# Pair steps of a four-round MLP dealt out by a timetable, with transposes moved into the next product

## The chip, the cores and the metric

The kernel runs on one core of a Trainium2 chip. The metric is the time of one execution on the device in microseconds (us); a row of runs is given by its median. A core has five engines that run side by side and wait for each other through semaphores: TensorE (matmuls and weight loads; PE and PEld in the profile), VectorE (DVE), ScalarE (ACT), GpSimd (POOL) and SyncE (SP), whose queue issues nearly all loads here. Each engine takes its instructions strictly in the order that was fixed when the program was built.

## The reference

Two layers of a decoder trunk for 256 tokens of width 2048, in float32:

```python
D_MODEL = 2048; SEQ = 256; DEPTH = 2; D_FF = 4 * D_MODEL
# each layer
h = rms(x, norm1_g)
z = h @ w_in                      # u | retention q,k,v,g | NSA | differential attention
x = x + concat([s5(u), retention(...), nsa(...), diff_attn(...)]) @ w_out
h2 = rms(x, norm2_g)
x = x + relu(h2 @ mlp_w1) ** 2 @ mlp_w2      # 2048 -> 8192 -> 2048
```

The change lies in the last line, the MLP.

## The kernel before

**Products.** The precision of float32 is kept with the type fp32r: each operand is split into a high part (a copy rounded on ScalarE) and a low part (VectorE subtracts the high part), and three matmuls stand for one: low x high, high x high, high x low. Weights come in chunks of 128 x 1024 (two blocks of 128 rows by 512 columns, 512 KB). `split_chunk` loads a chunk into one of four buffers `raw` (SP), writes `wh` (three buffers, ScalarE) and `wl` (two buffers, VectorE). `product_steps` gives a chunk 12 matmuls of 512 columns: for each of the two row blocks and each half of the tokens (t = 0, 1) two with `wh` and one with `wl`. Eight chunks make a product of 2048 rows by 512 columns in two accumulators of PSUM, `mm` (pool `ps`, four banks; the pool `pm` has four more, tag `ms`).

**The MLP.** It goes in four rounds. A round makes four blocks of 512 hidden columns from `h2` and `w1` (`first` half), transposes them into the slots `Bh`, `Bl` (`to_slots`: TensorE transposes 128 x 128, ScalarE writes `Bh`, VectorE writes `Bl`), and multiplies these slots with its quarter of `w2` in four output products (`second`), whose sums `residual` adds to x.

**Pairs.** Two of the four blocks of a round are made together with seven products in place of eight (Strassen's scheme in a form with few additions): `first_steps` makes the two that need no sums (accumulators p1, p2; 6 matmuls for each of 8 chunks), `sums_steps` the other five (p3 to p7; 15 matmuls for each of 8 steps). A step of `sums_steps` loads a chunk of each of the two blocks, subtracts them four times (`t13`, `t24`), and splits three results into `bh`/`bl`, `t13h`/`t13l`, `t24h`/`t24l`: ten instructions of VectorE and ScalarE for 15 matmuls. The sums of `h2` that these multiply were made once (`sums_slot`). `pair_last` combines the seven accumulators into four tiles. The other two blocks of a round are plain products.

**The order before.** `mix` runs two generators side by side. In round 0 the pair's 8 steps go between the 16 chunks of the two plain blocks, one to two chunks. In rounds 1 to 3 they go between the 32 chunks of the preceding round's output products, one to four chunks; then the pair is combined and transposed, and the two plain blocks follow, each with its Relu, Square and transposes at its end. The last round's output products run alone. A pair of blocks is made in every round.

The framework places instructions by priority: what is written inside `self.hp()` counts as if written 350 instructions earlier, and each engine's order is fixed when the program is built. `lhs[k]`, `h2`, `kt2` and `kh` are the transposed left sides. Names in the profile leave out buffer numbers; `p` stands for all of p1 to p7, `t` for `t13` and `t24`, `mo`, `c`, `v` for tiles of the mixers and of `pair_last`.

Of the kernel before, what the change touches and what calls it, by code (L numbers as in the profile page):

```python
# [54 lines left out]
class Trunk:  # L55
# [107 lines left out]
    def product_steps(self, out, chunks, lhs, n=512, before=None):  # L163
# [5 lines left out]
        for c, src in enumerate(chunks):  # L169
            if before:  # L170
                before(c)
            wh, wl = self.split_chunk(src, 2 * n, not before)
            mov = lambda w, j: w[:, j * n:(j + 1) * n]
            rows = lambda x, t: x[:, t * P:(t + 1) * P]
            for j in range(2):
                k = 2 * c + j
                xh, xl = lhs[k]
                for t in range(NT):
                    nc.tensor.matmul(acc[t], rows(xl, t), mov(wh, j), start=k == 0, stop=False)  # L179
                    nc.tensor.matmul(acc[t], rows(xh, t), mov(wh, j), start=False, stop=False)  # L180
            for j in range(2):
                k = 2 * c + j
                for t in range(NT):
                    nc.tensor.matmul(acc[t], rows(lhs[k][0], t), mov(wl, j), start=False, stop=k == nk - 1)  # L184
            if c == len(chunks) - 1:
                out.extend(acc)
            yield
# [50 lines left out]
    def sums_steps(self, out, chunks1, chunks2, slots, sums):  # L238
# [3 lines left out]
        acc = {i: self.pm.tile([P, 512], F32, name=f"p{i}", tag="ms") for i in (6, 7, 5, 3)}  # L242
        acc[4] = self.ps.tile([P, 512], F32, name="p4", tag="mm")
        last = len(chunks1) - 1
        f2 = lambda x: x.rearrange("p a b -> p (a b)")
        for c in range(last + 1):
            with self.hp():
                b1 = self.raw(chunks1[c]).rearrange("p (k n) -> p k n", k=2)
                b2 = self.raw(chunks2[c]).rearrange("p (k n) -> p k n", k=2)
                ta, tb = (self.wk.tile([P, 2, 512], F32, name=nm, tag="aux", bufs=2) for nm in ("t13", "t24"))  # L250
                V.tensor_tensor(ta[:, 0, :], b2[:, 0, :], b1[:, 0, :], ALU.subtract)  # L251
                V.tensor_tensor(ta[:, 1, :], b2[:, 1, :], b2[:, 0, :], ALU.subtract)  # L252
                V.tensor_tensor(tb[:, 0, :], b2[:, 1, :], ta[:, 0, :], ALU.subtract)
                V.tensor_tensor(tb[:, 1, :], tb[:, 0, :], b1[:, 1, :], ALU.subtract)  # L254
                bh = self.wk.tile([P, 512], F32R, name="bh", tag="z")
                bl = self.wk.tile([P, 512], F32R, name="bl", tag="w")
                ah = self.wp.tile([P, 1024], F32R, name="t13h", tag="wh", bufs=3)
                al = self.wp.tile([P, 1024], F32R, name="t13l", tag="wl", bufs=2)
                dh = self.wk.tile([P, 1024], F32R, name="t24h", tag=("Tq", "Tk")[c % 2], bufs=1)
                dl = self.wk.tile([P, 1024], F32R, name="t24l", tag=("s5b", "vones")[c % 2], bufs=1)  # L260
                for h, l, x in ((bh, bl, b2[:, 1, :]), (ah, al, f2(ta)), (dh, dl, f2(tb))):
                    nc.scalar.activation(h, x, AF.Copy)  # L262
                    V.tensor_tensor(l, x, h.bitcast(F32), ALU.subtract)  # L263
            half = lambda y, i: [v[:, i * 512:(i + 1) * 512] for v in y]
            S = lambda i: [x[:, i, :] for x in sums[c]]
            f = (c == 0, c == last)
            self.three(acc[3], S(3), (bh, bl), *f)
            self.three(acc[5], S(0), half((ah, al), 0), *f)
            self.three(acc[7], S(2), half((ah, al), 1), *f)
            self.three(acc[6], S(1), half((dh, dl), 0), *f)  # L270
            self.three(acc[4], [x[:, 1, P:] for x in slots[c]], half((dh, dl), 1), *f)
            if c == last:
                out.update(acc)
            yield
# [16 lines left out]
    def to_slots(self, src, cols, slots, j0, gain=None, sums=None, bank=None):  # L291

        nc = self.nc
        for jj in range(cols // 256):
# [9 lines left out]
            else:  # L304
                self.split_slot(pt, slots[j0 + jj], gain, 2 * (j0 + jj))
# [735 lines left out]
    def mlp(self, layer, h2, sums, r, ss, last):  # L1041


        nc = self.nc
        V = nc.vector
        kt2 = self.ktiles(h2)
        w1 = lambda rd, n: [self.ins["w1"][layer, 4 * rd + n, c] for c in range(8)]
        bank = lambda name: self.ps.tile([P, 512], F32, name=name, tag="mm")
        tmp = lambda nm, tag, n: self.wk.tile([P, 512], F32, name=nm, tag=tag, bufs=n)
        nxt = [None]  # L1050

        def mix(xs, ys, every, off):
            for i, _ in enumerate(xs):
                if i % every == off:
                    next(ys, None)
            for _ in ys:
                pass

        def pair_first(rd):
            p = []  # L1060
            for _ in self.first_steps(p, w1(rd, 0), h2):
                pass
# [48 lines left out]
        def both(gens):  # L1111
            for g in gens:
                yield from g
# [153 lines left out]
```

## Time and profile before

| | |
|---|---|
| median of 3 runs | 2340.57 us (2339.39 to 2343.62) |
| profiled execution: time, span in the trace | 2340.26 us, 2338.5 us |
| mean granted clock of TensorE | 0.991 |
| TensorE, VectorE, ScalarE busy | 97%, 72%, 53% of the span |
| loads | 439 MB, 189 GB/s over the span |
| first MLP, second MLP | about 430 to 1176 us, 1589 to 2335 us |

The busy time of an engine is the union of its instructions' spans. Matmuls overlap in the array, so that one of 512 columns has a span of 0.39 us while the next starts earlier; a busy TensorE is not one at its peak. The granted clock is a mean over the two levels that TensorE can have, 1.2 and 2.4 GHz (0.5 and 1.0).

### The profile page before, as it was taken

What the parts mean: (1) busy time and instruction counts of PE and PEld (TensorE: products, weight loads), DVE (VectorE), ACT (ScalarE), POOL (GpSimd) and SP (SyncE); (2) the same over time, 40 slices, a digit from 0 to 9 for tenths busy, and PEclk for the clock granted to TensorE, in tenths of its full rate; (3) what the DMA queues carried; (4) which work ended last, traced back from release to release, by engine and by line L of the source; (5) the groups of instructions that cost most, each with busy time, mean ns of one, the idle gap of its engine ahead of it and who ended that gap; (6) DMA issues with size and microseconds to landing.
All of it is one profiled execution on the core that took longest, in us unless ns stands there. A gap on an engine that the chain in (4) does not pass through costs nothing.

```text
span 2338.5 us, 29470 instructions
## 1 busy us (share of the span) xinstructions
PE 2259.8 (97%) x10540; PEld 1800.8 (77%) x10540; DVE 1690.3 (72%) x2545; ACT 1229.7 (53%) x1640; POOL 161.8 (7%) x396
## 2 busy tenths in 40 slices
PE   9999999999999999999999999999999999999999
PEld 7777778777877877777877777887778777777777
DVE  8988866887766766774569896668777667667644
ACT  6456544755455455454545665456554554554543
POOL 0213201200000000000002212102000000000000
PEclk9999999999999999999999999999999999999999
DMA  7544625666656656664554355356566566566554
GB/s 253 162 124 141 225 91 175 213 210 210 214 185 226 217 196 210 202 229 169 185 176 154 118 188 177 114 189 215 199 224 210 179 216 211 193 226 211 202 173 169
DMA packets 125139, 443.19 MB, mean 190 GB/s; under 512 B 15040, under 2 KB 15296, under 8 KB 124992
## 3 DMA queue, kind: packets, MB, share of 16 engines
q1 hardware_dynamic: 122400, 438.62, 55.6%
q10 hardware_dynamic: 2592, 2.70, 0.3%
q8 instruction: 82, 1.34, 0.2%
q14 instruction: 65, 0.53, 0.1%
HBM read 439.17 MB, written 2.10 MB: 189 GB/s over the span
## 4 chain that ended last, share of the span: by engine, by line
PE 68%; DVE 11%; DMA 10%; ACT 6%; issue 3%; POOL 3%; DVEq 0%; ACTq 0%; SPq 0%
PE mm L179 18%; PE mm L180 18%; PE mm L184 17%; DMA raw<-in_w_dram 9%; DVE wl L154 4%; PE p L221 3%; PE p L223 3%; PE p L222 3%; ACT wh L153 2%; PE tp L299 2%; ACT t13h L262 1%; ACT hid L1038 1%; DVE t L251 1%; PE bu L601 1%; DVE t L252 1%
## 5 line engine op out<-in xcount | busy, mean ns | idle before, releaser
L153 ACT ACTIVATE wh<-raw 128x1024 fp32r<-128x1024 f32 (+1 forms) x688 | 720.5, 1049 | 733.7 <-PE mm L180 478.8
L154 DVE TENSOR_TENSOR wl<-raw,wh 128x1024 fp32r<-128x1024 f32 (+1 forms) x688 | 830.5, 1211 | 380.3 <-PE mm L184 279.5
L179 PE MATMUL mm<-wh,Bl 128*128 128x512 f32 x1280 | 500.4, 391 | 2.9 <-ACT wh L153 1.9
L180 PE MATMUL mm<-wh,Bh 128*128 128x512 f32 x1280 | 500.1, 391 | 0.0
L179 PE MATMUL mm<-wh,Al 128*128 128x512 f32 (+1 forms) x1216 | 477.6, 394 | 5.6 <-ACT wh L153 3.6
L180 PE MATMUL mm<-wh,Ah 128*128 128x512 f32 (+1 forms) x1216 | 475.0, 392 | 0.0
L184 PE MATMUL mm<-wl,Ah 128*128 128x512 f32 (+1 forms) x1216 | 334.8, 395 | 11.4 <-DVE wl L154 11.1
L184 PE MATMUL mm<-wl,Bh 128*128 128x512 f32 x1280 | 344.8, 391 | 0.2 <-DVE wl L154 0.2
L179 PEld LDWEIGHTS mm<-wh,Bl 128*128 128x128 f32 x1280 | 240.3, 188 | 57.9 <-ACT wh L153 6.0
L180 PEld LDWEIGHTS mm<-wh,Bh 128*128 128x128 f32 x1280 | 240.4, 188 | 50.4
L184 PEld LDWEIGHTS mm<-wl,Ah 128*128 128x128 f32 x1216 | 223.3, 190 | 72.3 <-DVE wl L154 19.7
L184 PEld LDWEIGHTS mm<-wl,Bh 128*128 128x128 f32 x1280 | 239.3, 188 | 51.3 <-DVE wl L154 0.6
L179 PEld LDWEIGHTS mm<-wh,Al 128*128 128x128 f32 x1216 | 231.5, 190 | 59.5 <-ACT wh L153 8.5
L180 PEld LDWEIGHTS mm<-wh,Ah 128*128 128x128 f32 x1216 | 231.8, 191 | 50.3 <-issue 5.6
L262 ACT ACTIVATE bh<-raw 128x512 fp32r<-128x512 f32 x64 | 40.5, 633 | 181.9 <-DMA raw<-in_w_dram 181.9
L251 DVE TENSOR_TENSOR t<-raw 128x512 f32<-128x512 f32 x64 | 44.2, 691 | 94.0 <-DMA raw<-in_w_dram 94.0
L262 ACT ACTIVATE t13h<-t 128x1024 fp32r<-128x1024 f32 x64 | 67.8, 1060 | 47.6 <-DVE t L252 43.1
L263 DVE TENSOR_TENSOR t24l<-t,t24h 128x1024 fp32r<-128x1024 f32 x64 | 78.4, 1224 | 19.5 <-ACT t24h L262 19.1
L1033 DVE TENSOR_TENSOR x<-mm,x 128x512 f32<-128x512 f32 x96 | 61.9, 683 | 37.2 <-PE mm L184 37.0
L263 DVE TENSOR_TENSOR t13l<-t,t13h 128x1024 fp32r<-128x1024 f32 x64 | 77.9, 1218 | 0.2
L262 ACT ACTIVATE t24h<-t 128x1024 fp32r<-128x1024 f32 x64 | 67.0, 1047 | 5.5 <-DVE t L254 5.5
L312 DVE TENSOR_TENSOR Bl<-tp,Bh 128x512 fp32r<-128x512 f32 x76 | 48.9, 682 | 12.8 <-ACT Bh L311 12.8
(361 smaller groups left out, 2443.8 us busy)
## 6 DMA issues: line engine op xcount, KB each, us to landing
raw<-in_w_dram SPq DMA_DIRECT2D x576, 512.0 KB, 4.1
raw<-in_w_main_dram SPq DMA_DIRECT2D x160, 512.0 KB, 3.6
raw<-in_w_out_dram SPq DMA_DIRECT2D x64, 512.0 KB, 3.3
aux<-in_wcmp_dram SPq DMA_DIRECT2D x16, 512.0 KB, 5.0
raw<-in_w_gate_dram SPq DMA_DIRECT2D x16, 268.0 KB, 2.7
x<-in_x_dram SPq DMA_DIRECT2D x8, 256.0 KB, 5.0
aux<-in_s5g_dram SPq DMA_DIRECT2D x4, 512.0 KB, 4.4
out_dram<-x ACTq DMA_DIRECT2D x8, 256.0 KB, 2.1
```

Of the source, the lines that this page charges most:

```text
L153: self.nc.scalar.activation(h[:, :cols], r[:, :cols], AF.Copy)
L154: self.nc.vector.tensor_tensor(l[:, :cols], r[:, :cols], h[:, :cols].bitcast(F32), ALU.subtract)
L179: nc.tensor.matmul(acc[t], rows(xl, t), mov(wh, j), start=k == 0, stop=False)
L180: nc.tensor.matmul(acc[t], rows(xh, t), mov(wh, j), start=False, stop=False)
L184: nc.tensor.matmul(acc[t], rows(lhs[k][0], t), mov(wl, j), start=False, stop=k == nk - 1)
L221: nc.tensor.matmul(acc, xl, wh, start=first, stop=False)
L222: nc.tensor.matmul(acc, xh, wh, start=False, stop=False)
L223: nc.tensor.matmul(acc, xh, wl, start=False, stop=last)
L251: V.tensor_tensor(ta[:, 0, :], b2[:, 0, :], b1[:, 0, :], ALU.subtract)
L262: nc.scalar.activation(h, x, AF.Copy)
L263: V.tensor_tensor(l, x, h.bitcast(F32), ALU.subtract)
L1033: self.nc.vector.tensor_tensor(x, acc[t], x, ALU.add)
```

## The change

`mlp` is written anew around a timetable, `plan`: a list of all products of the MLP in order, each with the time of TensorE that its chunks are reckoned to take (2.72 us for a chunk of 12 matmuls, 1.36 for one of 6). The pair steps are a second stream. Each step is cut into five pieces, and one piece is let out after each 2.88 us of planned time, so that a step comes once in 14.4 us. The pairs are now blocks 4 and 5, 8 and 9, 12 and 13, 14 and 15: round 0 has four plain blocks, round 3 two pairs. There are four pairs in each MLP as before.

Further parts: `b1` and `b2`, the two chunks of a step, get one buffer each (the tags `Tk` and `vones`, which the mixers use) in place of two `raw` buffers each time, and `t24h`, `t24l` go from two buffers in turn to one; the pieces of a step have a priority of 250 in place of 350. The transposes of a plain block are written 5 us of planned time after its end, inside the next product, and those of a pair after the fourth and sixth chunk of an output product (for the last pair in part later). `apart` orders the first and the last chunk of a product so that the first accumulator's matmuls come before the second's. The order of the operations that combine a pair is changed.

```diff
-            for j in range(2):
-                k = 2 * c + j
-                xh, xl = lhs[k]
-                for t in range(NT):
...
+            for ts in ((0,), (1,)) if apart and c in (0, len(chunks) - 1) else (range(NT),):
+                for j in range(2):
+                    k = 2 * c + j
+                    xh, xl = lhs[k]
+                    for t in ts:
...
-    def sums_steps(self, out, chunks1, chunks2, slots, sums):
...
-                b1 = self.raw(chunks1[c]).rearrange("p (k n) -> p k n", k=2)
-                b2 = self.raw(chunks2[c]).rearrange("p (k n) -> p k n", k=2)
...
+    def sums_prep(self, out, src1, src2):
...
+        ahead = lambda: self.tc.high_priority(offset=self.prio - 100)
...
+        with ahead():
+            b1, b2 = (self.wk.tile([P, 2, 512], F32, name=nm, tag=tag, bufs=1) for nm, tag in (("b1", "Tk"), ("b2", "vones")))
+            nc.sync.dma_start(f2(b1), src1)
+            nc.sync.dma_start(f2(b2), src2)
+            ta, tb = (self.wk.tile([P, 2, 512], F32, name=nm, tag="aux", bufs=2) for nm in ("t13", "t24"))
+            V.tensor_tensor(ta[:, 0, :], b2[:, 0, :], b1[:, 0, :], ALU.subtract)
+            V.tensor_tensor(ta[:, 1, :], b2[:, 1, :], b2[:, 0, :], ALU.subtract)
+        yield
+        with ahead():
+            V.tensor_tensor(tb[:, 0, :], b2[:, 1, :], ta[:, 0, :], ALU.subtract)
+            V.tensor_tensor(tb[:, 1, :], tb[:, 0, :], b1[:, 1, :], ALU.subtract)
+        yield
+        with ahead():
+            bh = self.wk.tile([P, 512], F32R, name="bh", tag="z")
+            bl = self.wk.tile([P, 512], F32R, name="bl", tag="w")
+            split(bh, bl, b2[:, 1, :])
...
+        yield
+        with ahead():
+            dh = self.wk.tile([P, 1024], F32R, name="t24h", tag="Tq", bufs=1)
+            dl = self.wk.tile([P, 1024], F32R, name="t24l", tag="s5b", bufs=1)
+            split(dh, dl, f2(tb))
...
+        def plain(rd, n):
+            acc = []
+            yield from self.product_steps(acc, w1(4 * rd + n), kt2, apart=True)
...
+            at(now[0] + 5, lambda: place(rd, n, hs))
...
+        pairs = (4, 8, 12, 14)
...
+        put = lambda i, rd, n0: {3: lambda: place(rd, n0, ready[i][0]), 5: lambda: place(rd, n0 + 1, ready[i][1])}
+        N, W, A = 8 * [2.72], 8 * [2.72], 8 * [1.36]
+        plan = [(plain(0, n), N) for n in range(4)] + [(first(0, 4), A)]
+        plan += [(second(0, n, put(0, 1, 0) if n == 3 else {}), W) for n in range(4)]
+        plan += [(first(1, 8), A)] + [(plain(1, n), N) for n in (2, 3)]
...
+        gap = 14.4 / 5
+        due = gap
+        for xs, dts in plan:
+            for _, dt in zip(xs, dts):
+                now[0] += dt
+                while todo and todo[0][0] <= now[0]:
+                    heapq.heappop(todo)[-1]()
+                while due <= now[0]:
+                    due += gap
+                    next(ys, None)
+            next(xs, None)
```

What stands where is decided by the framework from these priorities, so three places of the built order are shown.

TensorE before, in layer 0: the end of the second plain block of round 1. `mm` are its two accumulators (L184), `tp` the transposes of its tiles `hid`, and `p` with `wh` and `wl` the first products of the next pair.

```order
L184 MATMUL mm_6449<-wl,Ah_3634 128x512
L184 MATMUL mm_6450<-wl,Ah_3634 128x512
L184 MATMUL mm_6449<-wl,Ah_3634 128x512
L184 MATMUL mm_6450<-wl,Ah_3634 128x512
L299 MATMUL tp<-ident,hid 128x128 x2
L221 MATMUL p_6615<-wh,Al_3621 128x512
```

TensorE of the change, the same two blocks of round 1, the next product under way on new accumulators, some chunks in; `p` with `t13h` is a pair step.

```order
L181 MATMUL mm_6681<-wh,Al_3625 128x512
L182 MATMUL mm_6681<-wh,Ah_3624 128x512
L181 MATMUL mm_6680<-wh,Al_3625 128x512
L182 MATMUL mm_6680<-wh,Ah_3624 128x512
L312 MATMUL tp<-ident,hid 128x128
L181 MATMUL mm_6681<-wh,Al_3625 128x512
L312 MATMUL tp<-ident,hid 128x128 x3
L182 MATMUL mm_6681<-wh,Ah_3624 128x512
L223 MATMUL p_5777<-t13h,Sl 128x512
L224 MATMUL p_5777<-t13h,Sh 128x512
L223 MATMUL p_5778<-t13h,Sl 128x512
L224 MATMUL p_5778<-t13h,Sh 128x512
```

Before, the transposes follow the block's last matmul. Now they stand among the third chunk of the next product: 26 wide matmuls are between the last one of the block that made `hid` and the first transpose.

VectorE before, one step in round 2's mixed stage: `t` the four subtractions (L251 to L254), `bl`, `t13l`, `t24l` the splits, `wl` those of product chunks.

```order
L251 TENSOR_TENSOR t_6875<-raw 128x512
L252 TENSOR_TENSOR t_6875<-raw 128x512
L154 TENSOR_TENSOR wl<-raw,wh 128x1024
L263 TENSOR_TENSOR bl<-raw,bh 128x512
L253 TENSOR_TENSOR t_6876<-raw,t_6875 128x512
L263 TENSOR_TENSOR t13l<-t_6875,t13h 128x1024
L254 TENSOR_TENSOR t_6876<-t_6876,raw 128x512
L154 TENSOR_TENSOR wl<-raw,wh 128x1024
L263 TENSOR_TENSOR t24l<-t_6876,t24h 128x1024
L154 TENSOR_TENSOR wl<-raw,wh 128x1024 x2
L251 TENSOR_TENSOR t_6988<-raw 128x512
```

VectorE of the change, one step among output products: L257 and L256 subtract from `b` (the tile `b2` first, then with `b1`), L260 and L261 make `t24`.

```order
L249 TENSOR_TENSOR t24l<-t_6705,t24h 128x1024
L249 TENSOR_TENSOR bl<-b_6862,bh 128x512
L155 TENSOR_TENSOR wl<-raw,wh 128x1024
L257 TENSOR_TENSOR t_6865<-b_6862 128x512
L256 TENSOR_TENSOR t_6865<-b_6862,b_6861 128x512
L155 TENSOR_TENSOR wl<-raw,wh 128x1024 x3
L249 TENSOR_TENSOR t13l<-t_6704,t13h 128x1024
L260 TENSOR_TENSOR t_6866<-b_6862,t_6865 128x512
L261 TENSOR_TENSOR t_6866<-t_6866,b_6861 128x512
L326 TENSOR_TENSOR Bl_6732<-tp,Bh_6731 128x512
L155 TENSOR_TENSOR wl<-raw,wh 128x1024
L249 TENSOR_TENSOR t24l<-t_6866,t24h 128x1024
```

The split `bl`, the last reader of a step's `b2`, moved from the middle of a step to its end, and one `wl` stands between it and the next step's first subtraction from a newly loaded `b`.

SP of the change, over about three steps: L254 loads `b2`, L253 loads `b1`, L141 the chunks into `raw`.

```order
L141 DMA raw<-in_w_dram 128x1024 x5
L254 DMA b_16583<-in_w_dram 128x1024
L253 DMA b_16582<-in_w_dram 128x1024
L141 DMA raw<-in_w_dram 128x1024 x5
L254 DMA b_16759<-in_w_dram 128x1024
L253 DMA b_16758<-in_w_dram 128x1024
L141 DMA raw<-in_w_dram 128x1024 x5
L254 DMA b_16890<-in_w_dram 128x1024
L253 DMA b_16889<-in_w_dram 128x1024
```

Before, this queue held loads of `raw` alone, those of pairs and of products; now each step's two loads stand in front of five to seven chunk loads.

## Rows read from the trace of the kernel before

**Rows 1.** The page: span, busy time of the engines, granted clock by slices.
```profile
span 2338.5 us, 29470 instructions
...
PE 2259.8 (97%) x10540; PEld 1800.8 (77%) x10540; DVE 1690.3 (72%) x2545; ACT 1229.7 (53%) x1640; POOL 161.8 (7%) x396
...
PEclk9999999999999999999999999999999999999999
```

**Rows 2.** Timeline of TensorE, 1120 to 1130 us (start, length, what).
```profile
1122.20 1.07 PE L184 MATMUL mm<-wl,Bh 128*128 128x512 f32 x4
...
1124.92 1.07 PE L184 MATMUL mm<-wl,Bh 128*128 128x512 f32 x4
...
1127.64 1.07 PE L184 MATMUL mm<-wl,Bh 128*128 128x512 f32 x4
```

**Rows 3.** First MLP by stages: length; PE, PEld, DVE, ACT, POOL; clock; DMA.
```profile
430.70:446.00 15.30, 12.41 (x54) 8.74 (x52) 15.25 (x27) 12.24 (x20) 8.42 (x2) 1.00 0.65 218
446.00:546.40 100.40, 94.33 (x398) 74.58 (x399) 81.71 (x97) 60.09 (x75) 4.89 (x12) 0.95 0.62 211
546.40:661.00 114.60, 113.70 (x490) 91.13 (x488) 86.19 (x96) 55.95 (x59) 0.00 (x0) 1.00 0.65 222
661.00:730.10 69.10, 64.44 (x288) 52.06 (x288) 38.91 (x42) 37.25 (x47) 0.00 (x0) 0.98 0.53 182
730.10:843.40 113.30, 112.93 (x488) 91.50 (x489) 85.13 (x95) 56.06 (x59) 0.00 (x0) 1.00 0.66 223
843.40:910.60 67.20, 62.70 (x290) 50.83 (x288) 39.24 (x42) 37.16 (x46) 0.00 (x0) 1.00 0.55 184
910.60:1030.80 120.20, 117.12 (x500) 93.37 (x501) 87.26 (x102) 58.15 (x63) 0.00 (x0) 1.00 0.65 222
1030.80:1086.00 55.20, 50.47 (x224) 40.57 (x224) 32.76 (x39) 30.23 (x41) 0.11 (x1) 0.97 0.54 185
1086.00:1176.00 90.00, 90.00 (x414) 74.87 (x415) 50.74 (x57) 42.68 (x59) 0.00 (x0) 1.00 0.54 184
```

**Rows 4.** The same view of the two MLPs whole.
```profile
430.70:1176.00 745.30, 718.09 (x3140) 577.66 (x3139) 517.18 (x591) 389.82 (x466) 13.42 (x15) 0.99 0.60 206
1589.00:2335.00 746.00, 719.49 (x3118) 576.18 (x3116) 503.86 (x559) 375.78 (x432) 11.88 (x14) 0.99 0.60 203
```

**Rows 5.** Timeline of all engines, 686 to 692 us, end of a plain block.
```profile
688.16 1.07 PE L184 MATMUL mm<-wl,Ah 128*128 128x512 f32 x4
...
689.37 1.25 ACT L1038 ACTIVATE hid<-mm,rb 128x512 f32<-128x512 f32 x2
...
690.51 1.14 ACT L1039 ACTIVATE hid<-hid 128x512 f32<-128x512 f32 x2
...
691.19 0.44 PE L299 MATMUL tp<-ident,hid 128*128 128x128 f32 x2 [1.96 <-ACT hid L1039]
```

**Rows 6.** Instructions by line: busy us, mean ns, idle us before them and releaser.
```profile
L299 PE MATMUL tp<-ident,hid 128*128 128x128 f32 x128 | 21.8, 297 | 30.0 <-ACT hid L1039 30.0
...
L251 DVE TENSOR_TENSOR t<-raw 128x512 f32<-128x512 f32 x64 | 44.2, 691 | 94.0 <-DMA raw<-in_w_dram 94.0
...
L154 DVE TENSOR_TENSOR wl<-raw,wh 128x1024 fp32r<-128x1024 f32 (+1 forms) x688 | 830.5, 1211 | 380.3 <-PE mm L184 279.5 <-issue 37.8 <-ACT wh L153 27.7
...
L263 DVE TENSOR_TENSOR t24l<-t,t24h 128x1024 fp32r<-128x1024 f32 x64 | 78.4, 1224 | 19.5 <-ACT t24h L262 19.1
...
L263 DVE TENSOR_TENSOR bl<-raw,bh 128x512 fp32r<-128x512 f32 x64 | 43.8, 684 | 0.0
...
L262 ACT ACTIVATE bh<-raw 128x512 fp32r<-128x512 f32 x64 | 40.5, 633 | 181.9 <-DMA raw<-in_w_dram 181.9
...
L1033 DVE TENSOR_TENSOR x<-mm,x 128x512 f32<-128x512 f32 x96 | 61.9, 683 | 37.2 <-PE mm L184 37.0
...
L312 DVE TENSOR_TENSOR Bl<-tp,Bh 128x512 fp32r<-128x512 f32 x76 | 48.9, 682 | 12.8 <-ACT Bh L311 12.8
```

**Rows 7.** Tile `raw`, 546 to 661 us: from issue to landing.
```profile
DMA to landing us min/median/max: 3.1/4.2/5.2
```

More of the change, by code (lines that the diff above doesn't have):

```diff
@@ L161, in product, with product_steps @@
         return acc
-    def product_steps(self, out, chunks, lhs, n=512, before=None):
+    def product_steps(self, out, chunks, lhs, n=512, before=None, apart=False):
         nc = self.nc
@@ new lines, in sums_prep @@
+        yield
[7 more added lines that the diff above has]
+            split(bh, bl, b2[:, 1, :])
+            ah = self.wp.tile([P, 1024], F32R, name="t13h", tag="wh", bufs=3)
+            al = self.wp.tile([P, 1024], F32R, name="t13l", tag="wl", bufs=2)
+            split(ah, al, f2(ta))
@@ L1045, in mlp @@
         V = nc.vector
-        kt2 = self.ktiles(h2)
[L1047 to L1057, printed above, removed]
@@ L1081, in pair_last, with second @@
                 self.act2(c21, c21, r, 1)
-            return (c11, c21), (c12, c22)
-        def plain(rd, n, hid):
+            ready[i] = (c11, c21), (c12, c22)
+        def second(rd, n, hooks={}):
             acc = []
-            yield from self.product_steps(acc, w1(rd, n), kt2)
-            with self.hp():
-                hs = []
-                for t in range(NT):
-                    hs.append(tmp("hid", "ev", 4))
-                    self.act2(hs[t], acc[t], r, t)
-                self.to_slots(lambda t: hs[t], 512, hid, 2 * n, bank=bank)
@@ L1133, in mlp @@
-        if not last:
-            nxt[0] = self.slots("A")
-        for _ in second(3, hid):
-            pass
-        return nxt[0]
+            for c, _ in enumerate(self.product_steps(acc, [self.ins["w2"][layer, rd, n, c] for c in range(8)],
+                                                     Lazy(slots[rd]), apart=True)):
+                if c in hooks:
+                    hooks[c]()
+                if c < 7:
+                    yield
+            self.residual(acc, n)
+            if rd == 3:
+                if last:
+                    for t in range(NT):
+                        nc.scalar.dma_start(self.out[t * P:(t + 1) * P, n * 512:(n + 1) * 512],
+                                            self.x[t][:, n * 512:(n + 1) * 512])
+                else:
+                    if n == 0:
+                        slots.append(self.slots("A"))
+                    with self.hp():
+                        self.to_slots(lambda t: self.x[t][:, n * 512:], 512, slots[4], 2 * n,
+                                      self.gains[:, 0, layer + 1])
+                        self.sumsq(ss, n)
@@ new lines, in second, with steps @@
+            yield
+        pairs = (4, 8, 12, 14)
+        def steps():
+            for i, b in enumerate(pairs):
+                p = {}
+                for c in range(8):
+                    w = []
+                    yield from self.sums_prep(w, w1(b)[c], w1(b + 1)[c])
+                    self.sums_step(p, w[0], h2[c], sums[c], c == 0, c == 7)
+                    if c == 7:
+                        combine(i, p)
+                    yield
+        put = lambda i, rd, n0: {3: lambda: place(rd, n0, ready[i][0]), 5: lambda: place(rd, n0 + 1, ready[i][1])}
@@ new lines, in mlp @@
+        plan += [(second(3, n, {} if n else {1: lambda: place(3, 3, ready[3][1])}), W) for n in range(4)]
+        ys = steps()
+        gap = 14.4 / 5
[9 more added lines that the diff above has]
+            next(xs, None)
@@ L1139, in run @@
+        assert next(ys, 0) == 0 and not todo
+        return None if last else slots[4]
     def run(self):
```

154 lines of the change are left out of this document (66 added, 88 removed).

## The prediction

> **What bounds the kernel now.** The page comes first: TensorE is busy 97% of the span, VectorE 72%, and the granted clock is at nine tenths or more in each slice [rows 1]. The busy time of overlapping matmuls does not tell how much is lost, so I counted instead. In the timeline of a stretch without transposes the last group of a weight chunk starts at 1122.20, 1124.92 and 1127.64 us [rows 2]: 2.72 us for 12 matmuls of 512 columns, 0.2267 us each, though one "takes" 0.39. In the last stage of the first MLP 414 matmuls take 90.0 us [rows 3]; 382 of them are 512 wide (86.6 us), so the 32 transposes took about 0.11 each.
>
> One MLP has 4 pairs x 168 + 8 plain blocks x 96 + 16 output products x 96 = 2976 wide matmuls, 674.7 us. With 160 transposes (17.6) in layer 0 and 128 (14.1) in layer 1, whose last products transpose nothing, TensorE needs 692.3 and 688.8 us. The MLPs take 745.3 and 746 us [rows 4], the second with a last microsecond behind its final matmul. Some 53 and 54 us, **107 us** in all, are waiting and half clock. The rest of the kernel is not touched.
>
> Where the 107 lie is read from the stages of the first MLP [rows 3], each as its length less its wide matmuls x 0.2267 less its transposes x 0.11:
> - 430.7 to 446, start: 46 wide and 8 transposes: 4 us lost.
> - 446 to 546.4, round 0, one pair step to two chunks: 366 and 32: 14 us; VectorE 81% busy, clock 0.95, so 5 of the 14 are clock.
> - the three mixed stages of rounds 1 to 3 (546.4, 730.1, 910.6), one step to four chunks: 4.0, 2.7 and 7.1 us, 0.58 per pair step.
> - the three hand-over stages (661, 843.4, 1030.8), two plain blocks and the next pair's first products: 7.5, 5.4, 7.6 us.
> - 1086 to 1176, output products alone: 0.0 us.
>
> The hand-overs have a clear wait. After the last matmul of a plain block (688.16 + 1.07 us) ScalarE takes two Relus and two Squares (689.37 to 691.65), and TensorE, whose next instruction is the transpose of `hid`, starts at 691.19 [rows 5]: 1.96 us idle, about 2.1 in starts. Over the kernel `hid` costs 30.0 us of idle time [rows 6], for 16 blocks. The half clock follows such gaps: (1 - clock) x length is 5.0, 1.4 and 1.7 us in the stages below full clock [rows 3].
>
> **The change part by part.** The numbers of matmuls, loads, splits and subtractions stay: four pairs in each MLP, and w1 is read as before.
>
> *Transposes inside the next product.* In the order, 26 wide matmuls of the next product stand between the end of a plain block and its first transpose, 5.9 us, against the 2.0 to 2.5 us that ScalarE needs. So the wait is hidden, with 3 us over for a chunk split that comes first on ScalarE. If that cover went, the 30 us would be back. The half clock that followed goes too.
>
> *Round 0 without a pair; steps spread.* A step now comes once in 14.4 us of other matmuls, 5.3 chunks, not 2 or 4. Round 0's 14 us go; the last output products, which stay unmixed, lose nothing, as in the last stage. `bh` now stands behind `t24h` on ScalarE, where before it waited 181.9 us for its load [rows 6] with chunk splits behind it.
>
> *Loads of their own.* `b1` and `b2` leave the four `raw` buffers, which then hold chunks alone, but have one buffer each. `b2` is read last by `bl`, so SP can issue the next `b2` only when `bl` is done, and `b1` and five chunk loads stand behind it on SP. On VectorE the order has none or one `wl` between that `bl` and the next step's subtraction of `b2`: the engine stands still for the load, with all later `wl` behind it, and TensorE waits for those. A load lands after 4.2 us (3.1 to 5.2) [rows 7]. Less a `wl` of 1.21, or none, VectorE waits 3.0 to 4.2 us a step; before it was 94.0 / 64 = 1.5 [rows 6].
>
> Does that fit? VectorE's work for a step [rows 6]: 5.3 `wl` 6.4, four subtractions 2.8, `bl` 0.7, `t13l` and `t24l` 2.4, and a 32nd of 11 residual pairs, 24 slot splits and 28 operations that combine, 1.6: 13.9 us. With 3.6 for the load and 0.3 for `t24h` (19.5 / 64) it is 17.8 us. TensorE's cycle is 14.4 + 15 x 0.2267 + 0.3 for transposes = 18.1. It fits with 0.3 us to spare, so TensorE will wait at times. Price of a step: from 0.0 (the last stage's loss) to 1.75 (14 us over 8 steps in round 0). I take 0.58, that of the mixed stages: density speaks for less, the longer stop of VectorE for more. 64 steps: 37 us.
>
> The Trainium skill's page "Trainium Kernel Development and Optimization" (Best Practices) asks for double buffers so that loads lie under compute, which speaks against one buffer each for `b1` and `b2`. The rows of before cannot show such a load; if all it adds to VectorE's wait (3.6 - 1.5 = 2.1 us) reached TensorE, 64 steps would cost 134 us more and the sum would end near 2425. I keep the 0.58, since two finished `wl` can lie ahead of TensorE.
>
> *First products.* There are still four a layer. The hand-overs less 2.1 for each of six blocks and 3.1 of clock leave (20.5 - 12.6 - 3.1) / 3 = 1.6 us for each. A step may now ride in them, where VectorE needs 1.21 for each 1.36 us of TensorE; that may add a microsecond, and belongs to the range. 8 x 1.6 = 13 us.
>
> *The start* stays at 4 to 5 us a layer (round 0 now opens with a plain block, which asks for half as many chunks, but VectorE still makes the sums of `h2`): 9 us. One step's subtractions move ahead into the retention gate; hidden by products there, some 4 us if not.
>
> *Last chunk by halves* (`apart`): the first accumulator ends six matmuls earlier, so one residual add of 0.68 us leaves the kernel's tail.
>
> Sum: 107 are replaced by 37 + 13 + 9 = 59: 48 less, and 0.7 of tail. The profiled execution took 2340.26 us (2338.5 of span and 1.8 around it), 0.3 below the median: 2340.3 - 49 = **2291 us**.
>
> **Rivals.** *A, the steps cost next to nothing.* For it: the last stage, where TensorE lost nothing with VectorE 56% busy, and chunks that have four `raw` buffers to themselves. Against it: VectorE's stop for `b2` in each cycle. At 0.1 a step, 6 + 13 + 9 = 28 remain: 2261 us.
>
> *B, slower: the load of `b2` sets the pace.* The cycle of `bl`, load, subtraction, splits and next `bl` has room for a load of 4.5 us; each microsecond above costs 64 us in all. A step then costs 0.58 + (landing - 4.5), and at (107 - 22) / 64 = 1.33 us the gain is gone: from a mean of 5.25 us. For it: `b2`, `b1` and waiting chunk loads are issued together, and single loads took 5.2 [rows 7]. Against it: the median of 4.2 was seen at the same density of traffic. At 5.5 us: 101 + 22 = 123, so 2357 us. The skill's rule on double buffers, above, would be right in this rival.
>
> *C, half of it.* The steps cost 1.0 each, because the stop of VectorE drains the two finished `wl` in the first products and at block ends: 64 + 22 = 86, 2319 us. The transposes' gain is then what is left.
>
> **Numbers.** Forecast 0.48 (own range 2272 to 2308), A 0.24, C 0.10, B 0.13, and 0.05 for a step price near 1.3, where nothing changes. A change below 0.2% (4.7 us) cannot be told from none. Faster 0.82 (forecast, A, C), same 0.05, slower 0.13. The range goes from just below A to beyond C: 2255 to 2330.
>
> **What would show it.** Idle time before the transposes of `hid` falls from 30.0 to under 4 us, and stages at clock 0.95 are gone. VectorE's wait for `b2` is 190 to 270 us over 64 steps. The mixed stretch loses about 0.6 us a step by count, the last output products none. I am wrong if TensorE waits above 1 us a step for `t13h`, `bl` or the `wl` behind them (B, C), if the `hid` wait comes back as one for accumulator banks, or if the splits keep up with no loss (A).

## The result and the profile after

The changed kernel takes 2278.78 us (median of 4 runs, 2275.82 to 2279.73), the one before 2339.98 us beside it: a ratio of 0.9737, 95% interval 0.9717 to 0.9757. That is 61 us less where 49 were forecast. The page of the changed kernel, beside [rows 1]:

```profile
span 2277.7 us, 29508 instructions
...
PE 2235.2 (98%) x10540; PEld 1794.8 (79%) x10540; DVE 1696.6 (74%) x2553; ACT 1226.9 (54%) x1640; POOL 151.3 (7%) x396
...
PEclk9999999999999999999999999999999999999999
```

The span is 60.8 us shorter. Windows of the first MLP, the mixers of layer 1 and the second MLP (here from the first matmul behind the mixers' output product to the last output product), and then the same mixers before:

```profile
436.70:1146.00 709.30, 704.28 (x3137) 573.20 (x3136) 516.08 (x586) 386.95 (x464) 8.10 (x15) 1.00 0.62 215
1146.00:1568.40 422.40, 409.89 (x2136) 323.45 (x2135) 323.43 (x618) 226.48 (x354) 65.15 (x176) 0.99 0.48 159
1568.40:2273.50 705.10, 701.00 (x3108) 569.40 (x3106) 502.41 (x554) 371.19 (x429) 7.66 (x14) 1.00 0.61 212
```

```profile
1177.70:1591.00 413.30, 405.56 (x2135) 320.57 (x2134) 321.38 (x613) 225.22 (x353) 67.77 (x176) 1.00 0.49 158
```

The MLPs took 745.1 and 743.0 us between the same marks before; they give 35.8 and 37.9 us. Less the 692.3 and 688.8 us of the forecast's count, 107 us of loss became 33. The half clock (the lower level of the granted clock, 0.5) went with it: summed over both MLPs, (1 - clock) x length was 18.8 us before and is 0.0. But the stretch ahead of the first MLP is 4.1 us longer (432.6 to 436.7). In the kernels below TensorE has the order of before there for at least its first 1839 of 2162 instructions, and the stretch took 432.4 to 436.0 us, so that this much varies from trace to trace. The mixers of layer 1 are 9.1 us longer, though the change does not touch them.

Six of the stages of the first MLP (start; plain blocks with steps; the first product of pair 0; output products with steps; the first product of pair 1; the end), to be read like [rows 3]:

```profile
434.60:450.00 15.40, 15.40 (x73) 12.79 (x72) 14.43 (x28) 12.09 (x20) 7.19 (x12) 1.00 0.43 155
450.00:545.00 95.00, 95.00 (x427) 77.67 (x427) 67.13 (x75) 52.63 (x63) 0.79 (x3) 1.00 0.63 215
545.00:566.90 21.90, 20.53 (x94) 16.42 (x93) 18.22 (x20) 15.22 (x19) 0.00 (x0) 1.00 0.77 255
566.90:678.70 111.80, 111.80 (x496) 91.15 (x494) 84.47 (x97) 56.83 (x64) 0.00 (x0) 1.00 0.63 215
678.70:693.00 14.30, 13.01 (x53) 9.31 (x53) 10.52 (x10) 7.61 (x8) 0.00 (x0) 1.00 0.75 254
1030.40:1144.00 113.60, 113.60 (x530) 94.30 (x529) 72.44 (x87) 58.83 (x80) 0.00 (x0) 1.00 0.54 186
```

By the forecast's count the start lost 0.0 us, the two long stages with steps 1.2 and 1.7, the first products 2.0 and 2.7, the end 0.4. Where length and busy time are equal, no idle time is left in TensorE's records. A matmul that starts late by less than the overlap (a span of 0.39 us, the next one 0.2267 later) does not show there, so the losses go by the count. The granted clock is 1.00 in each of them, where [rows 3] has 0.95. The groups by line that answer to [rows 6]:

```profile
L155 DVE TENSOR_TENSOR wl<-raw,wh 128x1024 fp32r<-128x1024 f32 (+1 forms) x688 | 829.7, 1211 | 317.0 <-PE mm L186 210.9 <-issue 41.9 <-ACT wh L154 32.0
L154 ACT ACTIVATE wh<-raw 128x1024 fp32r<-128x1024 f32 (+1 forms) x688 | 715.9, 1048 | 756.1 <-PE mm L182 527.6 <-DMA raw<-in_w_dram 80.8 <-DVE wl L155 43.5
...
L249 DVE TENSOR_TENSOR bl<-b,bh 128x512 fp32r<-128x512 f32 x64 | 43.9, 686 | 6.3 <-ACT bh L248 6.0
L256 DVE TENSOR_TENSOR t<-b,b 128x512 f32<-128x512 f32 x64 | 43.8, 685 | 6.7 <-DMA b<-in_w_dram 6.6
...
L248 ACT ACTIVATE bh<-b 128x512 fp32r<-128x512 f32 x64 | 40.4, 631 | 39.6 <-DMA b<-in_w_dram 39.0
...
L312 PE MATMUL tp<-ident,hid 128*128 128x128 f32 x128 | 20.1, 272 | 0.0
```

The transposes of `hid` wait for nothing. Over all 64 steps VectorE stands 6.7 us before L256, the subtraction that reads both `b2` and `b1`, and ScalarE 39.6 before `bh`. And `wh`, which waited 132.3 us for its load before, now waits 80.8:

```profile
L153 ACT ACTIVATE wh<-raw 128x1024 fp32r<-128x1024 f32 (+1 forms) x688 | 720.5, 1049 | 733.7 <-PE mm L180 478.8 <-DMA raw<-in_w_dram 132.3 <-DVE wl L154 43.8
```

### The profile page after: what moved, and what is told of

It reads as the page before. It is cut to its first block, busy times and chain, and to the rows that moved or that the text cites. A ratio compares the mean times of both kernels' runs of the same rounds, so it can differ in the third digit from the quotient of the medians.

```text
span 2277.7 us, 29508 instructions
## 1 busy us (share of the span) xinstructions
PE 2235.2 (98%) x10540; PEld 1794.8 (79%) x10540; DVE 1696.6 (74%) x2553; ACT 1226.9 (54%) x1640; POOL 151.3 (7%) x396
## 3 DMA queue, kind: packets, MB, share of 16 engines
q8 instruction: 83, 1.36, 0.2%
## 4 chain that ended last, share of the span: by engine, by line
PE 83%; DVE 7%; DMA 3%; POOL 3%; ACT 2%; issue 2%; DVEq 0%; ACTq 0%; SPq 0%
PE mm L186 22%; PE mm L181 22%; PE mm L182 22%; PE p L225 4%; PE p L223 4%; PE p L224 4%; DVE wl L155 2%; DMA raw<-in_w_dram 2%; PE tp L312 2%; ACT wh L154 1%; PE yp L643 1%; DMA aux<-in_wcmp_dram 1%; PE glu L664 1%; PE bu L615 1%; POOL rst L90 1%
## 5 line engine op out<-in xcount | busy, mean ns | idle before, releaser
L248 ACT ACTIVATE bh<-b 128x512 fp32r<-128x512 f32 x64 | 40.4, 631 | 39.6 <-DMA b<-in_w_dram 39.0
L325 ACT ACTIVATE Bh<-tp 128x512 fp32r<-128x512 f32 x76 | 43.6, 587 | 30.1 <-PE tp L312 29.5
```

## The experiments

Twelve kernels ran, beside runs of the kernel before with medians of 2340.0 to 2341.6 us; "lost" is what the two MLPs took beyond 692.3 + 688.8 us, as above. It and the mixers are read from one profiled execution, which can lie up to 5 us from the median beside it (2311.4 us for loads in `raw`, 2322.6 for transposes alone).

```
kernel                              median   ratio [95%]              lost  mixers 1
before                              2340.0   1                        107   413.3
changed                             2278.8   0.9737 [0.9717, 0.9757]   33   422.4
spread alone                        2332.6   0.9965 [0.9947, 0.9982]   94   418.6
transposes alone                    2318.0   0.9901 [0.9888, 0.9915]   81   419.1
own loads alone                     2322.3   0.9918 [0.9896, 0.9941]   83   416.6
changed, transposes at block end    2308.3   0.9854 [0.9841, 0.9867]   62   419.8
changed, loads in raw               2307.2   0.9855 [0.9842, 0.9869]   74   418.4
changed but for the spread          2284.4   0.9755 [0.9730, 0.9779]   48   413.9
changed, raw, bh on GpSimd          2311.1   0.9873 [0.9847, 0.9899]   72   418.1
changed, b2 loaded twice            2290.5   0.9787 [0.9755, 0.9819]   46   421.7
changed, no steps in first products 2278.1   0.9730 [0.9708, 0.9753]   34   423.7
changed, first step no priority     2278.8   0.9732 [0.9719, 0.9746]   34   421.6
changed, first step held            2275.2   0.9712 [0.9688, 0.9735]   34   422.5
the last, two wl on GpSimd          2288.0   0.9771 [0.9745, 0.9798]   46   422.2
```

**Transposes at the block's end.**

```diff
-            at(now[0] + 5, lambda: place(rd, n, hs))
+            place(rd, n, hs)
```

> The changed kernel (2279 us), with the transposes of a plain block's hid written again at the block's end, in front of the next product; all else as changed. Theory 1, the wait for hid is a main part of the gain: the idle time before these transposes, 30.0 us in the kernel before, comes back, with 2 to 6 us of half clock behind it: 2309 to 2315 us. Rival, the gain is the even spread of the steps and their matmuls now fill that gap as well: idle time under 8 us, at most 2287 us.

2308.3 us: 29.5 more, 0.7 below theory 1's range. The group in this kernel:

```profile
L181 PE MATMUL mm<-wh,Al 128*128 128x512 f32 (+1 forms) x1216 | 472.6, 390 | 7.7 <-DVE Bl L326 4.3 <-ACT wh L154 3.2
...
L223 PE MATMUL p<-wh,Al 128*128 128x512 f32 x128 | 51.8, 404 | 6.4 <-DVE Bl L326 4.3 <-ACT wh L154 2.0
...
L312 PE MATMUL tp<-ident,hid 128*128 128x128 f32 x128 | 19.9, 278 | 13.8 <-ACT hid L1053 13.8
```

Only 13.8 us stand before the transposes. Another 8.6 (4.3 and 4.3) stand before the next product's first matmuls, which now wait for the slot split `Bl` of those transposes. The part is worth what was forecast, though not all of it in the row where it was looked for. Why these transposes wait 13.8 us here and 30.0 before, no run shows: the halves of the last chunk (`apart`), which end the first accumulator sooner, are still in this kernel.

**Transposes alone.** The kernel before, whose blocks put off their `to_slots` until the third chunk of the next product (`if c == 2 and late: late.pop()()` after each chunk).

> The kernel before (2340 us) with one part of the change alone: the transposes of hid written behind the third chunk of the next product (for the last block of a round, of the next first product), the steps dealt, loaded and ordered as before. Theory 1: it takes away the 30.0 us of idle time and the clock behind it, 3 to 5 us: 2305 to 2310 us, so about half of the 61 us. Rival, the spread of the steps is nearly all of it: 2330 us or more.

2318.0 us: 23 less, between the two. The wait before these transposes is 0.0 us in its rows, and 26 us of loss are gone, but its layer 1 mixers are 5.8 us longer.

**Loads in the shared buffers.**

```diff
-            b1, b2 = (self.wk.tile(..., tag=tag, bufs=1) for nm, tag in (("b1", "Tk"), ("b2", "vones")))
-            nc.sync.dma_start(f2(b1), src1)
-            nc.sync.dma_start(f2(b2), src2)
+            b1 = self.raw(src1).rearrange("p (k n) -> p k n", k=2)
+            b2 = self.raw(src2).rearrange("p (k n) -> p k n", k=2)
```

> The changed kernel with b1 and b2 loaded into the four raw buffers that the chunks use, as in the kernel before. Theory 2, buffers of their own are what makes a step cheap, since the two loads of a step hold raw buffers for most of a step and the chunks starve: the price of a step goes from about 0.2 us back towards the 0.58 of before: 64 x 0.38 = 24, 2295 to 2303 us. Rival, the spacing of the steps alone makes them cheap, and a chunk load at 2.7 us for each buffer is far ahead in any case: within 4 us of 2279.

2307.2 us: theory 2, and past its range. In the profiled execution 41 us of loss come back, while the mixers of layer 1 and the stretch ahead of the first MLP are 4 us shorter each. ScalarE in this kernel:

```profile
L154 ACT ACTIVATE wh<-raw 128x1024 fp32r<-128x1024 f32 (+1 forms) x688 | 720.3, 1050 | 732.7 <-PE mm L182 364.8 <-DMA raw<-in_w_dram 206.2 <-DVE wl L155 48.9
...
L248 ACT ACTIVATE bh<-raw 128x512 fp32r<-128x512 f32 x64 | 40.5, 633 | 187.5 <-DMA raw<-in_w_dram 187.5
```

It waits 394 us for loads, `wh` and `bh` together, against 120 in the changed kernel. The next run is to part the two. That the pool was shared is not told apart from its size: no run gave `b1`, `b2` and the chunks one pool of six buffers.

**The same, `bh` written by GpSimd.**

```diff
+            if h is bh:
+                nc.gpsimd.tensor_copy(h, x)
+            else:
+                nc.scalar.activation(h, x, AF.Copy)
-            nc.scalar.activation(h, x, AF.Copy)
```

> The kernel with b1 and b2 in the shared raw buffers (2307.2 us), with bh written by GpSimd, which stands idle in the MLP, in place of ScalarE, so that ScalarE no longer stands at bh for b2's load (187.5 us there, 39.6 in the changed kernel) with the chunks' wh behind it. Theory 1, that stop is how the shared buffers cost 28 us: it is back at 2279 to 2288. Theory 2, the four shared buffers themselves are too few, a chunk's load is issued late because a step holds two of them, and wh waits for its own load (206 us there, 81 in the changed kernel): 2300 to 2312 us.

2311.1 us: theory 2. Its groups:

```profile
L154 ACT ACTIVATE wh<-raw 128x1024 fp32r<-128x1024 f32 (+1 forms) x688 | 720.4, 1050 | 935.0 <-PE mm L182 365.0 <-DMA raw<-in_w_dram 357.3 <-DVE wl L155 46.3
...
L249 POOL CAST bh<-raw 128x512 fp32r<-128x512 f32 x64 | 67.4, 1053 | 1096.4 <-DMA raw<-in_w_dram 790.1 <-DVE wl L155 184.1 <-DVE Bl L329 52.6
...
L260 DVE TENSOR_TENSOR t<-raw 128x512 f32<-128x512 f32 x64 | 60.2, 941 | 0.0
...
L259 DVE TENSOR_TENSOR t<-raw 128x512 f32<-128x512 f32 x64 | 50.2, 784 | 38.8 <-DMA raw<-in_w_dram 38.2
```

ScalarE no longer stands at `bh`, but `wh` waits 357.3 us for its own load where it waited 206.2: nothing is won. That speaks for theory 2, in which the chunks' loads come late when a step holds two of the four buffers. It is not a clean proof, since GpSimd's copy brought a cost of its own: the two subtractions L259 and L260 keep VectorE busy 22 us longer than with `bh` on ScalarE (the last section has those rows).

**Own loads alone.** The kernel before with `b1` and `b2` as in the change, and one buffer each for `t24h` and `t24l`.

> The kernel before with one part of the change alone: b1 and b2 in single buffers of their own, t24h and t24l in one buffer each, steps dealt as before (one to two chunks in round 0, one to four in the rounds 1 to 3). Theory A, the four raw buffers left to the chunks are worth what they were worth to the changed kernel, 28 us, wherever the steps stand: 2308 to 2318 us. Rival, the single buffer needs the spread: at one step to two chunks in round 0 the load of 4.3 us is waited for in each, and only the rounds 1 to 3 gain: 2330 us or more.

2322.3 us: 19 less, between the two; 24 us of loss are gone. The eight steps of round 0 (117 of their 120 matmuls), before and in this kernel, and its ScalarE:

```profile
446.00:525.00 79.00, 76.67 (x325) 61.15 (x326) 66.01 (x78) 44.68 (x53) 4.89 (x12) 0.98 0.64 218
```

```profile
449.20:524.20 75.00, 74.23 (x325) 60.21 (x326) 63.89 (x75) 44.37 (x53) 6.32 (x13) 1.00 0.67 233
```

```profile
L153 ACT ACTIVATE wh<-raw 128x1024 fp32r<-128x1024 f32 (+1 forms) x688 | 717.9, 1049 | 815.9 <-PE mm L180 666.4 <-DVE wl L154 33.3 <-DMA raw<-in_w_dram 25.9
...
L263 ACT ACTIVATE bh<-b 128x512 fp32r<-128x512 f32 x64 | 40.0, 625 | 25.9 <-DMA b<-in_w_dram 25.9
```

With 317 and 316 wide matmuls and 8 transposes the stretch lost 6.3 us before, 1.7 of them half clock, and loses 2.5 here, at the same one step to two chunks: 0.32 a step in place of 0.80. Of what these steps cost, the loads were the larger part, not the density. The other 7.6 of round 0's 14 us lie behind its steps. In round 3, at one step to four chunks, this kernel lost 1.6 us over its steps (461 wide matmuls), 0.2 a step:

```profile
913.60:1019.70 106.10, 106.10 (x462) 86.66 (x461) 78.46 (x91) 52.01 (x56) 0.11 (x1) 1.00 0.64 215
```

**Spread alone.** Both edits of the changed kernel shown above, together.

> The changed kernel with both other parts undone: transposes of hid at the block's end and b1, b2 in the shared raw buffers. What is left of the change is the spread of the steps (none in round 0) and the last chunks by halves. Undone singly, the two parts cost 29 us (2308.3) and 28 us (2307.2). Theory A, the parts add and the spread by itself is worth next to nothing: 2279 + 29.5 + 28.5 = 2337, within 6. Rival, the forecast's view that the spread takes away the 14 us of round 0 and that part of the 28 and 29 is one and the same: 2305 to 2325 us.

2332.6 us: theory A. What is left of the change, the even spread above all, is worth 8.5 us by itself; with it stay the halves, the lower priority of the steps and the new order of combining, which no run tried singly.

**All but the spread.** The kernel before with both other parts.

> The kernel before with the transposes of hid inside the next product and b1, b2 in buffers of their own, but its dealing of the steps (round 0 with a pair, one step to two chunks there). Alone the two parts gave 23 us (2318.0) and 19 us (2322.3). Theory A, they add, and their meeting with the spread gives the rest of the 62: 2341 - 42 = 2299, within 5. Rival 1, the two need each other, since freed chunk loads matter most where nothing else stops TensorE, and the spread is worth its 9 us alone: 2284 to 2292. Rival 2, the transposes inside the next product take the slack that the dense steps need: 2305 or more.

2284.4 us: rival 1. Alone the two parts give 23 and 19 us, together 56, which is 14 more than their sum. In the MLPs they take away 26 and 24 us of loss alone and 59 together, 9 more than the sum; the rest lies outside, since this kernel has the short mixers and those with one part have longer ones. With both in place the spread takes another 14 us of loss out of the MLPs, but its kernel has the longer mixers, and the net is 5.6 us between the medians, with intervals that overlap. The mixers here:

```profile
1150.60:1564.50 413.90, 406.00 (x2135) 321.10 (x2134) 324.68 (x618) 226.26 (x354) 68.94 (x176) 1.00 0.51 162
```

Where the spread does its work is read from the loss of both MLPs by their parts, counted with the wide matmuls and transposes in each part:

```
                          first 20 us   next 90   the rest
before                       12.1         26.0      68.9
spread alone                  4.6          4.8      84.4
changed but for the spread   10.2         13.7      23.6
changed                       0.4          2.6      30.7
```

It wins in the first 110 us of an MLP. In the first MLP 1.6 first products and the eight steps of round 0 stood there before, and 6.5 steps with hardly a matmul of a first product stand there now. It pays a part of that back in the rest, which now holds 4 first products and 25.5 steps in place of 2.4 and 24.

**`b2` loaded twice.**

```diff
+            nc.sync.dma_start(f2(b2), src1)
             nc.sync.dma_start(f2(b2), src2)
```

> The changed kernel in which each b2 buffer is loaded twice, one load behind the other (the first with b1's data, overwritten by the second), so that b2 lands a load, some 3 to 4.3 us, later in each of the 64 steps, and b1 and the chunk loads behind it on SP as well. Rival B of the prediction (the load sets the pace, each microsecond above a landing of 4.5 us costs 64 us): with a landing of 8 us or more 64 x 3.5 = 224 more, some 2500 us. Other theory: b2's buffer comes free at the second pair of subtractions (it was read wrongly in the forecast: the bl before the first subtraction is of the same step), with two or three wl and a t24l ahead of the next use, and VectorE and ScalarE have 3 to 4 us of slack in a cycle of 18: the load's delay eats the slack and costs up to 1 us a step: 2285 to 2345 us.

2290.5 us: the other theory, at its low end. SyncE issues the second load 3.3 us behind the first, in one step of this kernel (SyncE, then VectorE, then the groups):

```profile
601.28 0.33 SPq L254 DMA_DIRECT2D b<-in_w_dram  x1
...
604.62 0.33 SPq L255 DMA_DIRECT2D b<-in_w_dram  x1
```

```profile
610.74 0.69 DVE L257 TENSOR_TENSOR t<-b,b 128x512 f32<-128x512 f32 x1 [2.41 <-DMA b<-in_w_dram]
```

```profile
L257 DVE TENSOR_TENSOR t<-b,b 128x512 f32<-128x512 f32 x64 | 44.2, 691 | 68.4 <-DMA b<-in_w_dram 66.5 <-issue 1.5 <-DVE wl L155 0.3
...
L248 ACT ACTIVATE bh<-b 128x512 fp32r<-128x512 f32 x64 | 40.4, 632 | 146.6 <-DMA b<-in_w_dram 146.4
```

The subtraction now starts 9.5 us after the first issue. VectorE waits 1.07 us a step and ScalarE 2.3, and the MLPs lose 12.5 us more than in the changed kernel, 0.2 a step.

**No steps in the first products.**

```diff
+                due += dt if dts is A else 0
-        gap = 14.4 / 5
+        gap = 13.2 / 5
```

> The changed kernel with no step pieces in the first products of a pair (the clock of the steps stands still there, and a step comes every 13.2 us elsewhere instead of 14.4). By count the eight first products and what borders on them lose about 2.2 us each, 17 of the 34 us that are left in the MLPs. Theory, it is the riding steps that VectorE has no room for at 1.21 us of split for each 1.36 us of TensorE: the first products lose under 1 us each and the kernel takes 2266 to 2272 us. Rival, a first product alone is too dense for VectorE and the slot splits of the block before it, whatever rides: 2277 to 2284.

2278.1 us: the rival by its time. Counted from the first to the last of their matmuls, the eight first products lose 13.4 us here and 18.0 in the changed kernel, 1.7 and 2.3 each, so the pieces that ride in them do cost something there. But the loss of the MLPs is the same (34 and 33): with the steps 1.2 us closer elsewhere, the other stages lose what the first products gain.

**The first step without priority, and held back.** The first takes `high_priority` from the first step's preparation; the second writes one column of `h2`'s first slot into `b1` and `b2` on GpSimd ahead of their loads.

> The changed kernel without priority for the preparation of each layer's first pair step, so that its loads and subtractions stay in the MLP. Between the MLPs the changed kernel lost 3.8 us (layer 0) and 8.9 us (layer 1) against the kernel before. Theory 3, this is the step that moved ahead into the retention gate: the two stretches go back to 430.8 and 413.4 us, within 2, and the kernel takes 2266 to 2273 us. Rival, the layer 1 mixers are ordered otherwise for other reasons, or clock: at most 3 us of change, 2276 to 2282.

2278.8 us, but this tells nothing of theory 3: its subtractions still stood in the retention gate, as in the changed kernel, where a `wl` stands behind the wait for the norm:

```profile
1489.18 0.69 DVE L256 TENSOR_TENSOR t<-b,b 128x512 f32<-128x512 f32 x1 [1.45 <-DMA b<-in_w_dram]
...
1491.00 1.22 DVE L155 TENSOR_TENSOR wl<-raw,wh 128x1024 fp32r<-128x1024 f32 x1
...
1494.59 2.64 DVE L934 TENSOR_SCALAR mo<-rpv,bmv,brs 128x128 f32<-128x128 f32 x8 [1.78 <-POOL brs L931]
1497.15 1.22 DVE L155 TENSOR_TENSOR wl<-raw,wh 128x1024 fp32r<-128x1024 f32 x1
```

> The changed kernel with the loads of each layer's first pair step held back until the first slot of h2 is written (a one-column copy on GpSimd into b1 and b2 ahead of the loads), so that no subtraction of a step stands in the retention gate. Without priority alone they still stood there. Theory 3, in layer 1 the hoisted subtractions push a chunk's wl behind VectorE's wait for the retention norm: TensorE's gap of 2.4 us near 350 us of the layer 1 mixers and the half clock window behind it, 1.7 us, go: mixers of layer 1 from 422.3 to 417.5 to 419, the kernel 2273 to 2276 us. Rival, that gap comes from the norm itself and stays: 2278 to 2281.

2275.2 us, the fastest median, though not told apart from the changed kernel's by their intervals. The gap is gone from TensorE (2.04 us idle before a `wl` matmul in the changed kernel at 1498.42 us, 0.17 at most there now), and one stretch of half clock with it (1.7 us), but this profile's layer 1 mixers are as long as ever (422.5), and its 4 us of shorter span lie in front of and in the first MLP. Theory 3 does not explain the mixers.

**Two of eight `wl` of a first product on GpSimd**, in the kernel with the first step held.

> The changed kernel with the first step held back from the retention gate (2275.2 us), and the wl of two of the eight chunks of each first product written by GpSimd in place of VectorE. Theory, the 2 us that each of the eight first products loses are VectorE's (eight wl of 1.21 in 10.9 us of TensorE, with slot splits, and what rides or waits behind): 2.4 us less there save 1 to 2 us each: 2259 to 2268 us. Rival, GpSimd's subtraction is so long (no row has one of this size; its rows of 512 columns take 0.7 to 1.0 us for another operation) that the matmuls wait for it: 2276 us or more.

2288.0 us: the rival, 13 us slower than without it:

```profile
L155 DVE TENSOR_TENSOR wl<-raw,wh 128x1024 fp32r<-128x1024 f32 (+1 forms) x672 | 825.3, 1233 | 330.3 <-PE mm L186 223.8 <-issue 38.5 <-ACT wh L154 26.3
...
L225 PE MATMUL p<-wl,Ah 128*128 128x512 f32 x128 | 44.3, 415 | 15.2 <-POOL wl L155 7.9 <-DVE wl L155 7.3
...
L155 POOL TENSOR_TENSOR wl<-raw,wh 128x1024 fp32r<-128x1024 f32 x16 | 40.2, 2511 | 959.8 <-PE p L225 482.6 <-ACT wh L154 470.9 <-DVE wl L155 6.3
```

One such subtraction takes 2.51 us on GpSimd against 1.21, and the matmuls of the first products that read `wl` wait 15.2 us where they waited 2.6.

## Why the prediction was right, and where its steps were not

The time lies in the range, and faster was right, but that it lies so near the 2291 us is partly luck, since two errors partly cancel: 59 us of loss were to be left in the MLPs and 33 are; and 13 us came back outside, of which the text had named 4.

**Transposes: right.** The 30.0 us of [rows 6] are 0.0, no part of either MLP is below full clock, and undoing the part costs 29.5 us. The clock is not the transposes' alone: with them as the one change (1 - clock) x length is 6.8 us over both MLPs, with own loads as the one change 10.2, with both 0.0, against 18.8 before.

**Loads of their own: wrong in sign.** The text said that VectorE would wait 190 to 270 us for `b2`; it waits 6.7. The step that failed is the reading of the order, that `b2` is read last by `bl`. VectorE's and SyncE's timeline of one cycle of the changed kernel:

```profile
605.89 0.68 DVE L249 TENSOR_TENSOR bl<-b,bh 128x512 fp32r<-128x512 f32 x1
606.49 0.69 DVE L256 TENSOR_TENSOR t<-b,b 128x512 f32<-128x512 f32 x1
607.09 0.69 DVE L257 TENSOR_TENSOR t<-b 128x512 f32<-128x512 f32 x1
...
615.02 0.69 DVE L260 TENSOR_TENSOR t<-b,t 128x512 f32<-128x512 f32 x1
615.75 0.69 DVE L261 TENSOR_TENSOR t<-t,b 128x512 f32<-128x512 f32 x1
617.45 1.22 DVE L155 TENSOR_TENSOR wl<-raw,wh 128x1024 fp32r<-128x1024 f32 x1 [1.01 <-PE mm L186]
618.60 1.22 DVE L249 TENSOR_TENSOR t24l<-t,t24h 128x1024 fp32r<-128x1024 f32 x1
619.73 0.68 DVE L249 TENSOR_TENSOR bl<-b,bh 128x512 fp32r<-128x512 f32 x1
```

```profile
615.74 0.33 SPq L254 DMA_DIRECT2D b<-in_w_dram  x1
616.47 0.33 SPq L253 DMA_DIRECT2D b<-in_w_dram  x1
```

The `bl` at 605.89 is of the same step as the subtractions behind it. The order printed ahead of the forecast shows the same: its `bl` and the L257, L256 and L260 behind it all read `b_6862`, so `bl` was not the last reader there. The last reader is L260, and `b2`'s next load is issued as it ends, at 615.74. Until the next `bl`, at 619.73, VectorE has L261, a `wl` and a `t24l` to do, and the load lands meanwhile. The forecast put `b2`'s load between `bl` and the subtraction, which both read the same `b2`, landed before either. The Trainium skill's page "Trainium Kernel Development and Optimization" (Best Practices) asks for double buffers; by it the sum was 2425 us. The trace does not agree here: a single buffer cost VectorE 0.1 us a step, and with a further load behind each the kernel lost 12 us. What counted was the side that the forecast left unpriced: four `raw` buffers for the chunks alone. With them taken away the kernel is 28 us slower.

**A step at 0.58: too dear.** The eight first products, with the pieces that ride in them, lost 18.0 us of the 33 (counted from the first to the last of their matmuls), which leaves 15, or 0.24 a step, nearer to rival A's 0.1. The 0.58 was taken from stages in which the steps used the shared buffers; that price was largely one of loads: with own loads alone, and the steps as close as before, it is 0.2 in round 3 and 0.32 in round 0. The upper price of 1.75 was read too high as well, since round 0's steps held 6.3 of the 14 us.

**Round 0's 14 us and the start's 9:** both gone. With own loads and moved transposes, but the pair still in round 0, 13.7 of the 26.0 us in the two stretches behind the starts are left (table above), and 2.6 without the pair: about half went for the stated reason, half with the loads and the `hid` waits. The start went against the forecast, which left it standing because of the sums of `h2`: 10.2 us with a first product at the start, 0.4 with a plain block there.

**First products at 1.6: about right without riders.** They lose 1.7 us each without pieces of steps in them and 2.3 with; the microsecond that riding steps may add had been left to the range. The last chunks by halves were not tried by themselves.

**The mixers of layer 1: not seen.** The scheduler lists them anew when the MLP ahead of them changes. Counted in the traces, the matmuls of products that stand before the fifth of eight groups of `yp`, and the length of the mixers:

```
603 matmuls: before 413.3, own loads alone 416.6, all but the spread 413.9
669 matmuls: transposes at block end 419.8, two wl on GpSimd 422.2
671 matmuls: the other nine 418.1 to 423.7
```

Each kernel with the order of before is shorter there than each with another. The clock is a part of it: (1 - clock) x length over these mixers is 0.0 to 1.7 us in the first three and 3.4 to 5.1 in the eleven others, 5.1 of the changed kernel's 9.1 us. That the order costs the 5 to 10 us is read from these 14 traces; no run forced one order on the other kernel, and why a changed MLP brings one or the other stays open. Among the last nine, those with own loads have 421.6 to 423.7 and the others 418.1 to 419.1; the kernel whose first step is held back, without the gap in the gate, has 422.5, so that gap is not what parts them.

## What to carry to other kernels

Price an edit of buffers on both sides: what the moved load waits for, and what the buffers that it leaves free let the others do. Before a wait is forecast from an order, find for each reader of the buffer which turn of the loop it belongs to. Before the gains of parts are added or compared, look at the stretches that no part touches: of the 14 us by which two parts gave more together (56) than alone (23 and 19), only 9 lay where they work. Those 9 fit a stretch that is held by whichever wait is left, though no run shows it stage by stage.

## What the runs showed of the hardware

VectorE slows beside GpSimd. With `bh` on GpSimd the two subtractions of 512 columns that mostly run beside its copy, L259 and L260, took 784 and 941 ns in the mean, as the rows above show. Of L260's 64, the 40 that overlap a copy took 1098 ns and the 24 others 680. With the same loads and `bh` on ScalarE the two took

```profile
L255 DVE TENSOR_TENSOR t<-raw 128x512 f32<-128x512 f32 x64 | 44.2, 690 | 41.3 <-DMA raw<-in_w_dram 40.9
...
L256 DVE TENSOR_TENSOR t<-raw 128x512 f32<-128x512 f32 x64 | 43.8, 685 | 0.0
```

690 and 685 ns. The Trainium skill's page "Perfetto Trace Analysis" (Optimizing Scalar/DVE Operations) says that the two engines share a read port, so that moving work between them might not help. The traces agree that it might not help: VectorE slows only in the overlap, and the kernel with 16 `wl` on GpSimd lost 13 us, though there GpSimd's own 2.51 us for what VectorE does in 1.21 stand behind the loss as well. That a port is the reason, no run here shows.
